# Expert products half in split fp32r parts, half in native fp32, with other buffers, one-hots and pacing

## The chip, the cores and the metric

The kernel runs on one core of a Trainium2 chip. It is judged by the device time of one execution in microseconds (us). A plain run gives one such time; a run with the hardware profiler gives one as well, and with it the span from the first to the last instruction and the trace that the rows below are taken from.

## The reference

One layer of a transformer for 256 tokens of width 2048, in fp32: two attention branches (a low-rank one and a differential one), gates, an output projection, and then an expert mixer. The change lies in the mixer alone. Its 16384 experts stand on a grid of 128 rows and 128 columns. Each token picks 16 experts in each of 8 heads, by two top-16 lists and a top-16 of their sums, and takes

```
h = rmsnorm(x, g_norm2)
...                                   # row, col, gates of 8 x 16 experts a token
experts = row * PEER_NKEYS + col
a = gelu(einsum('chkd,cd->chk', expert_u[experts], h))
w = gates * a
out = einsum('chk,chkd->cd', w, expert_v[experts])
```

`expert_u` and `expert_v` are 16384 x 2048 fp32, 134 MB each.

## The kernel before

**Stages.** Attention, gates and projections come first (0 to 810 us of the profile). Then the U stage (810 to 1520 us), then the V stage (1520 to 2147 us). For 192 of the 256 tokens (TD) the mixer is dense: every expert's product with every token is made, and a gate matrix that is zero where a token did not pick the expert is multiplied in. For the other 64 tokens (TG) the chosen rows are gathered from HBM: 128 gathers of 128 rows of 8 KB, 64 of U and 64 of V, spread over both stages.

**U stage.** A loop over 128 blocks of 128 experts. A block is one matrix of 2048 x 128 (1 MB), fetched in two tiles of 512 KB. `u_mm` multiplies it in 16 k tiles of 128 rows into one PSUM bank: the block's tile is the stationary operand, the normalized tokens `h2` (192 columns) the moving one. Both are plain fp32, which TensorE takes as it is ("native"). `u_evac` then applies Gelu on ScalarE from PSUM into `Blow` or `Bhigh`, which keep all 128 blocks. A one-element copy on VectorE, `pace`, marks that the block is done; gathers are tied behind it (`gather_to`).

**Work beside the blocks.** Three routing steps a block (top-16 lists, candidates, indices; VectorE) run from block 2 on. After half of them the gathers start. From block C0 = 32 on, 48 gate steps `g_step` are spread over the matmuls by GRATE: each multiplies, for 4 tokens, a one-hot matrix R of the rows (GpSimd) with a one-hot matrix C of the columns times the gates (VectorE), 4 matmuls of 128 columns, and VectorE multiplies the result into `Blow` and `Bhigh` or copies it there. GU = 80/128 of the gathers lie in the U stage. A gather's 128 rows are multiplied with `hrep` (U) or added to `gacc` (V) by one instruction on VectorE, and the buffer's next gather is issued on GpSimd behind it; there are two such buffers.

**Fetching and splitting.** Weights elsewhere, and all of V, are taken in two parts: `split` has ScalarE round a fetched tile `raw` to fp32r (`hi`), and VectorE subtract it (`lo`); fp32r matmuls of `hi` and `lo` follow. `fetch` gives such a tile one of three `raw` buffers, or for every fourth tile a fourth one. All fetches stand on one queue, SP's, in a fixed order; an issue that waits for a buffer holds up those behind it. In the U stage nothing is split, so `fetch_whole` uses the idle `hi` and `lo` buffers for fetches too: ten buffers of 512 KB, five blocks.

The order of instructions on an engine is set when the program is built; each engine, and SP's queue, works through its own list in order.

Of the kernel before, what the change touches and what calls it, by code (L numbers as in the profile page):

```python
# [7 lines left out]
F32 = mybir.dt.float32  # L8
F32R = mybir.dt.float32r
U32 = mybir.dt.uint32  # L10
AF = mybir.ActivationFunctionType
ALU = mybir.AluOpType
# [5 lines left out]
KD = D // 128  # L18
# [4 lines left out]
TD = 192  # L23
TG = T - TD
NLOW = 64
C0 = 32
NG4 = TD // 4
GRATE = NG4 / (88 * 16)
NEG = -1.0e30
NEGBIG = -3.0e38  # L30

# [1 line left out]
def hybrid_peer(tc, a, out):  # L33
    nc = tc.nc
    es = ExitStack()

    def pool(stack, name, bufs=1, side=None, space=None):
        kw = {} if space is None else dict(space=space)
        return stack.enter_context(
            tc.tile_pool(name=name, bufs=bufs, side=side, reuse_waits="tile", **kw))  # L40

    cst = pool(es, "cst")
    st = pool(es, "st")

    ident = cst.tile([128, 128], F32, name="ident")
    iota = cst.tile([128, 128], F32, name="iota")
    ones = cst.tile([128, 1], F32, name="ones")
    nhalf = cst.tile([128, 2], F32, name="nhalf")

    state = {"n": 0, "max": 3, "fill": 0, "b": 0, "g": 0, "c": 0, "f": 0, "s": 0, "w": 0}  # L50
    st2 = []


    def fetch(src):
        state["f"] += 1
        p, n = (st2[0], 1) if st2 and state["f"] % 4 == 3 else (st, 3)
        raw = p.tile([128, 1024], F32, tag="raw", name="raw", bufs=n)
        nc.sync.dma_start(raw, src)
        return raw

    def fetch_whole(src):

        i = state["w"] % (10 if st2 else 8)
        state["w"] += 1
        tag, n = (("raw", 3), ("hi", 3), ("lo", 2), ("raw", 3), ("hi", 3), ("raw", 3), ("hi", 3),
                  ("lo", 2), ("raw", 1), ("lo", 1))[i]
        p = st2[0] if i > 7 else st
        raw = p.tile([128, 1024], F32 if tag == "raw" else F32R, tag=tag, name="raw", bufs=n)
        raw = raw.bitcast(F32) if tag != "raw" else raw
        nc.sync.dma_start(raw, src)  # L70
        return raw

    def split(raw):

        hi = st.tile([128, 1024], F32R, tag="hi", name="hi", bufs=3)
        nc.scalar.activation(hi, raw, AF.Copy)  # L76
        state["s"] += 1
        p, n = (st2[0], 1) if st2 and state["s"] % 3 == 2 else (st, 2)
        lo = p.tile([128, 1024], F32R, tag="lo", name="lo", bufs=n)
        state["lo"] = nc.vector.tensor_sub(lo, raw, hi.bitcast(F32)).ins  # L80
        return hi, lo
# [36 lines left out]
    def tick(n=1):  # L118
        state["n"] += n
        if state["n"] >= TICK:  # L120
            state["n"] -= TICK
            advance()
# [48 lines left out]
    def ps_blk(n=3):  # L171
        state["b"] += 1
        return bank(f"b{state['b'] % n}")

    def ps_s():
        return pp.tile([128, 512], F32, tag="s", name="s", bufs=2)

    def ps_m():
        return pp.tile([128, 512], F32, tag="m", name="m", bufs=1)

    def w1(name, tag, bufs=2):
        return wk.tile([128, T], F32, tag=tag, name=name, bufs=bufs)
# [51 lines left out]
    g1, g2 = small[:, 0:16], small[:, 16:32]  # L234
# [157 lines left out]
    ps = ps_s()  # L392
# [23 lines left out]
    for h in range(NH):  # L416
        ps = ps_blk()
# [4 lines left out]
    for j in range(NH // 2):  # L422
        ps = ps_blk()
# [90 lines left out]
    for h in range(NH):  # L514
        ps = ps_blk()
# [55 lines left out]
    for b in range(32):  # L571
        ps = ps_blk()
# [15 lines left out]
    for j in range(KD):  # L588
        m = []
        for u, o, b in ((u_oa, oTa, j), (u_ob, oTb, 16 + j)):  # L590
            ps = ps_blk()
            block(u, o, NH, ps)
            mm = w1("mm", "rb", 3)
            nc.vector.scalar_tensor_tensor(mm, gt[:, b], 1.0, total(mm, ps),
                                           op0=ALU.add, op1=ALU.mult)
# [9 lines left out]
    gw = pool(gws, "gw", side="right")  # L605
    rowT = gw.tile([128, 2, 128], F32, name="rowT")
    colT = gw.tile([128, 2, 128], F32, name="colT")
    gateT = gw.tile([128, 2, 128], F32, name="gateT")

    hrep = gw.tile([128, D], F32, name="hrep")  # L610
    gidx = gw.tile([128, 64], U32, name="gidx")
# [5 lines left out]
    nc.gpsimd.tensor_add(sel[:, 64:128], ident[:, 0:64], ident[:, 64:128])  # L617
    h2s = ExitStack()
    h2p = pool(h2s, "h2p", side="right")
    h2 = h2p.tile([128, KD, TD], F32, name="h2")  # L620


    scs = ExitStack()
# [18 lines left out]
    def r2_job():  # L642
        yield
        v = nm.col()
        yield
        nc.scalar.activation(r2, nm.row(v), AF.Copy)
        yield
        for q in range(4):
            pt = ps_m()
            for i in range(4):  # L650
                k = 4 * q + i
                hn = w1("hn", "on", 3)
                nc.vector.tensor_mul(hn, xT[:, k], r2)
                nc.scalar.activation(h2[:, k], hn[:, 0:TD], AF.Copy, scale=g2[:, k:k + 1])
                hg = wk.tile([128, 2, TG], F32, tag="hg", name="hg", bufs=2)
                nc.gpsimd.tensor_scalar(hg, hn[:, TD:].unsqueeze(1).broadcast_to([128, 2, TG]),
                                        g2[:, k:k + 1], None, op0=ALU.mult)
                nc.tensor.transpose(pt[:, i * 128:(i + 1) * 128],
                                    hg.rearrange("p a t -> p (a t)"), ident)
                if i % 2:  # L660
                    yield
            nc.scalar.activation(hrep[:, q * 512:(q + 1) * 512], pt, AF.Copy)

    for j in range(KD):
        ps = ps_blk()
# [23 lines left out]
    for b in range(16):  # L689
        ps = ps_blk()  # L690
        block(u_wq, hu, KD, ps)
        job(score_job(b, ps))
    fill = []
    u_raw = []


    def u_mm(ps):
        for k in range(KD):
            if k % 8 == 0:
                u_raw.append(fetch_whole(a["eu"][len(u_raw)]))  # L700
            mm = nc.tensor.matmul(ps[:, 0:TD], lhsT=u_raw[-1][:, k % 8 * 128:(k % 8 + 1) * 128],  # L701
                                  rhs=h2[:, k], start=(k == 0), stop=(k == KD - 1),
                                  skip_group_check=True)
            state["u"] = mm.ins
            if active or queue:
                state["mm"] = mm.ins
                tick()
            state["fill"] += len(fill) > 0
            while fill and state["fill"] * GRATE >= NG4 + 1 - len(fill):
                fill.pop(0)()  # L710
# [14 lines left out]
    utp = pool(bs, "utp")  # L725
# [19 lines left out]
    for tb in (1, 0):  # L745
# [58 lines left out]
        def r_tr(env=env, tb=tb):  # L804
            pg = ps_g()
            for n, key in enumerate((0, 1, "g")):
                nc.tensor.transpose(pg[:, n, :], env[key].rearrange("p h k -> p (h k)"), ident)
            for n, dst in enumerate((rowT, colT, gateT)):
                nc.vector.tensor_copy(dst[:, tb, :], pg[:, n, :])

        steps.append(r_alloc)
        steps += [lambda b=b, f=r_list: f(b) for b in range(16)]
# [69 lines left out]
    def u_evac(c, ps):  # L882

        b = Bsl(c, c + 1)[:, 0]
        n = 4 * state["g"]
        if n < TD:
            nc.scalar.activation(b[:, n:], ps[:, n:TD], AF.Gelu_apprx_tanh)
        if n:
            t = utp.tile([128, TD], F32, tag="ut", name="ut", bufs=2)
            nc.scalar.activation(t[:, 0:n], ps[:, 0:n], AF.Gelu_apprx_tanh)  # L890
            nc.gpsimd.tensor_mul(b[:, 0:n], b[:, 0:n], t[:, 0:n])  # L891
        state["c"] = c + 1
        pace = utp.tile([128, 1], F32, tag="pace", name="pace", bufs=2)
        state["pace"] = nc.vector.tensor_copy(pace, b[:, TD - 1:TD] if n < TD else ps[:, 0:1]).ins  # L894

# [2 lines left out]
    def onehots(t4):  # L900
        rc = []
        for i in range(4):
            tb, tt = divmod(4 * t4 + i, 128)
            R = gp.tile([128, 128], F32, tag="R", name="R", bufs=12)
            C = gp.tile([128, 128], F32, tag="C", name="C", bufs=12)
            row, col, gate = [x[:, tb, tt:tt + 1] for x in (rowT, colT, gateT)]
            nc.gpsimd.tensor_scalar(R, iota, row, None, op0=ALU.is_equal)  # L907
            nc.vector.tensor_scalar(C, iota, col, gate, op0=ALU.is_equal, op1=ALU.mult)  # L908
            rc.append((R, C))
        RC[t4] = rc  # L910

# [17 lines left out]
                nc.vector.tensor_copy(bv, g)  # L929
        state["g"] += 1  # L930

    GU0, GU = 14, 80 / 128
    for c in range(C0):
        ps = ps_u() if c else ps0
        if c:
            u_mm(ps)
        u_evac(c, ps)
        for _ in range(3):
            if steps and c > 1:
                steps.pop(0)()  # L940
                if len(steps) == 34:
                    gather()
                    gather()
        gather_to(max(0, c - GU0) / (NB - GU0) * GU, state["pace"])
# [9 lines left out]
    fill += [lambda t4=t4: g_step(t4) for t4 in range(NG4)]  # L954
    for c in range(C0, NB):
        ps = ps_u()
# [84 lines left out]
    for half in range(2):  # L1041
# [17 lines left out]
        for c in range(NB):  # L1059
            raw = fetch(a["ev"][half, c])  # L1060
            hl = split(raw)
            parts = [[p[:, q * 512:(q + 1) * 512] for p in hl] for q in range(2)]
            w = weights(c)
# [143 lines left out]
```

## Time and profile before

| | |
|---|---|
| median of 3 runs | 2153.38 us (2150.89 to 2154.23) |
| profiled execution, its own time | 2148.66 us |
| its span | 2146.9 us |
[...]
| TensorE, VectorE, ScalarE, GpSimd busy | 98%, 67%, 37%, 27% of the span |

The page of the profile gives the busy time of each engine over the span, and again in 40 slices, in tenths. The chain of waits follows the work that ended last back to the start. Views of one line or one stretch give the durations of its instructions, what they waited for, and, for fetches, the time from issue to landing.

### The profile page before, as it was taken

What the parts mean: (1) busy time and instruction counts of PE and PEld (TensorE: products, weight loads), DVE (VectorE), ACT (ScalarE), POOL (GpSimd) and SP (SyncE); (2) the same over time, 40 slices, a digit from 0 to 9 for tenths busy, and PEclk for the clock granted to TensorE, in tenths of its full rate; (3) what the DMA queues carried; (4) which work ended last, traced back from release to release, by engine and by line L of the source; (5) the groups of instructions that cost most, each with busy time, mean ns of one, the idle gap of its engine ahead of it and who ended that gap; (6) DMA issues with size and microseconds to landing.
All of it is one profiled execution on the core that took longest, in us unless ns stands there. A gap on an engine that the chain in (4) does not pass through costs nothing.

```text
span 2146.9 us, 30521 instructions
## 1 busy us (share of the span) xinstructions
PE 2099.1 (98%) x11438; PEld 1864.9 (87%) x11438; DVE 1441.8 (67%) x2468; ACT 788.8 (37%) x1304; POOL 579.2 (27%) x525
## 2 busy tenths in 40 slices
PE   7989999999999999999999999999999999999998
PEld 6877778888888889999999999999888888788886
DVE  7666658666876798644555555554688878788874
ACT  3434437555554541100000000000355555555554
POOL 4121110000002302234666676663211111111100
PEclk9999999999999999999999999999999999999999
DMA  5453453455556557799888888888888888888874
GB/s 186 168 172 132 138 185 129 152 191 187 192 186 215 184 178 265 231 356 328 317 311 318 315 313 320 313 316 307 313 331 307 321 316 305 305 328 316 305 290 148
DMA packets 132708, 546.78 MB, mean 255 GB/s; under 512 B 15120, under 2 KB 15696, under 8 KB 116048
## 3 DMA queue, kind: packets, MB, share of 16 engines
q1 hardware_dynamic: 112032, 404.60, 53.0%
q0 software_dynamic: 18560, 134.29, 16.7%
q10 hardware_dynamic: 1968, 5.94, 0.9%
q8 instruction: 90, 1.47, 0.3%
q14 instruction: 58, 0.48, 0.1%
HBM read 537.89 MB, written 4.19 MB: 252 GB/s over the span
## 4 chain that ended last, share of the span: by engine, by line
PE 88%; DMA 2%; DVE 1%; issue 0%; ACT 0%; POOL 0%; ACTq 0%; DVEq 0%; POOLq 0%; SPq 0%
PE b L701 16%; PE b L137 15%; PE s L999 8%; PE b L139 8%; PE n L701 8%; PE m L701 8%; PE m L999 5%; PE n L999 5%; PE b L999 4%; PE t L999 4%; PE s L917 2%; DMA raw<-in_ev 1%; DVE lo L80 1%; PE b L156 1%; PE b L157 1%; PE b L155 1%
## 5 line engine op out<-in xcount | busy, mean ns | idle before, releaser
L80 DVE TENSOR_TENSOR lo<-raw,hi 128x1024 fp32r<-128x1024 f32 x502 | 635.0, 1270 | 269.7 <-ACT hi L76 129.7
L76 ACT ACTIVATE hi<-raw 128x1024 fp32r<-128x1024 f32 x502 | 531.9, 1061 | 537.1 <-PE n L999 139.2
L701 PE MATMUL b<-h,raw 128*128 128x192 f32 x2048 | 342.0, 326 | 0.0
L701 PEld LDWEIGHTS b<-h,raw 128*128 128x128 f32 x2048 | 333.1, 190 | 0.0
L137 PE MATMUL b<-xg,hi 128*128 128x512 f32 x912 | 328.0, 402 | 2.7 <-DVE xg L187 1.5
L139 PE MATMUL b<-xg,lo 128*128 128x256 f32 x912 | 259.2, 284 | 12.1 <-DVE lo L80 12.1
L137 PEld LDWEIGHTS b<-xg,hi 128*128 128x128 f32 x912 | 173.8, 191 | 46.6 <-issue 4.9
L999 PE MATMUL s<-hi,wt 128*128 128x512 f32 x512 | 203.1, 397 | 0.0
L139 PEld LDWEIGHTS b<-xg,lo 128*128 128x128 f32 x912 | 174.6, 191 | 14.0 <-DVE lo L80 13.8
L701 PE MATMUL n<-h,raw 128*128 128x192 f32 x1024 | 173.3, 326 | 0.0
L701 PE MATMUL m<-h,raw 128*128 128x192 f32 x1024 | 173.3, 326 | 0.0
L842 POOL DMA_INDIRECT rows<-in_evn,gidx x64 | 85.9, 1342 | 306.0 <-DVE gacc L860 276.2
L701 PEld LDWEIGHTS m<-h,raw 128*128 128x128 f32 x1024 | 166.9, 190 | 0.0
L701 PEld LDWEIGHTS n<-h,raw 128*128 128x128 f32 x1024 | 166.9, 190 | 0.0
L855 DVE SCALAR_TENSOR_TENSOR rows<-rows,hrep 128x2048 f32<-128x2048 f32 x64 | 148.7, 2324 | 14.3 <-DMA rows<-in_eun,gidx 14.3
L860 DVE SCALAR_TENSOR_TENSOR gacc<-rows,gwt,gacc 128x2048 f32<-128x2048 f32 x63 | 148.2, 2353 | 0.6 <-DVE pace L894 0.6
L907 POOL TENSOR_SCALAR R<-iota,rowT 128x128 f32<-128x128 f32 x192 | 136.0, 720 | 42.6 <-PE s L917 40.6
L842 POOL DMA_INDIRECT rows<-in_eun,gidx x64 | 75.8, 1184 | 255.6 <-DVE rows L855 196.3
L891 POOL TENSOR_TENSOR Bhigh<-Bhigh,ut 128x192 f32<-128x192 f32 (+28 forms) x64 | 97.9, 1529 | 88.6 <-ACT ut L890 81.2
L999 PEld LDWEIGHTS s<-hi,wt 128*128 128x128 f32 x512 | 96.3, 188 | 23.8 <-issue 0.5
L908 DVE TENSOR_SCALAR C<-iota,colT,gateT 128x128 f32<-128x128 f32 x192 | 62.9, 380 | 60.6 <-PE s L917 60.3
L999 PE MATMUL b<-hi,wt 128*128 128x512 f32 x256 | 102.1, 399 | 0.6 <-DVE wt L984 0.6
(316 smaller groups left out, 3502.9 us busy)
## 6 DMA issues: line engine op xcount, KB each, us to landing
raw<-in_eu SPq DMA_DIRECT2D x256, 512.0 KB, 5.4
raw<-in_ev SPq DMA_DIRECT2D x256, 512.0 KB, 4.6
raw<-in_w_in SPq DMA_DIRECT2D x133, 512.0 KB, 3.7
raw<-in_w_out SPq DMA_DIRECT2D x32, 512.0 KB, 4.3
raw<-in_w_q SPq DMA_DIRECT2D x32, 512.0 KB, 3.8
raw<-in_w_o_mla SPq DMA_DIRECT2D x16, 512.0 KB, 4.3
raw<-in_w_o_diff SPq DMA_DIRECT2D x16, 512.0 KB, 4.3
raw<-in_w_uq SPq DMA_DIRECT2D x9, 512.0 KB, 4.4
```

The costliest lines, as they stand in the source:

```text
L76: nc.scalar.activation(hi, raw, AF.Copy)
L80: state["lo"] = nc.vector.tensor_sub(lo, raw, hi.bitcast(F32)).ins
L137: nc.tensor.matmul(ps[0:m, 0:512], lhsT=hi, rhs=act[:, k, :], start=(k == 0), stop=False)
L139: state["mm"] = nc.tensor.matmul(ps[0:m, 0:256], lhsT=lo, rhs=act[:, k, 0:256], start=False, stop=(k == nk - 1)).ins
L701: mm = nc.tensor.matmul(ps[:, 0:TD], lhsT=u_raw[-1][:, k % 8 * 128:(k % 8 + 1) * 128], rhs=h2[:, k], start=(k == 0), stop=(k == KD - 1), s ...
L842: nc.gpsimd.indirect_dma_start(out=g, out_offset=None, in_=a["eun" if which == "u" else "evn"], in_offset=bass.IndirectOffsetOnAxis(ap=gid ...
L855: nc.vector.scalar_tensor_tensor(g, g, 1.0, hrep, op0=ALU.mult, op1=ALU.mult, accum_out=gdot[:, j:j + 1])
L860: nc.vector.scalar_tensor_tensor(gacc, g, gwt[:, j:j + 1], gacc, op0=ALU.mult, op1=ALU.add)
L891: nc.gpsimd.tensor_mul(b[:, 0:n], b[:, 0:n], t[:, 0:n])
L907: nc.gpsimd.tensor_scalar(R, iota, row, None, op0=ALU.is_equal)
L908: nc.vector.tensor_scalar(C, iota, col, gate, op0=ALU.is_equal, op1=ALU.mult)
L999: nc.tensor.matmul(o, lhsT=l, rhs=r, start=first and i == 0, stop=last and i == len(ops) - 1, skip_group_check=True)
```

## The change

- Of each block's 16 k tiles, the lower 8 (the first tile of 512 KB) are split by `split` and multiplied in two fp32r passes: `hi` with the high and low part of the tokens side by side (`h2hl`, 384 columns), `lo` with the high part (192 columns). The upper 8 stay native. PSUM then holds 384 columns a block.
- `u_evac` therefore copies the second 192 columns out on ScalarE (`us`), adds the first on VectorE, and takes Gelu from there. That add takes the place of `pace`.
- `fetch_whole` goes. U's fetches use `fetch`: the three `raw` buffers and the fourth.
- The token parts of k 0 to 7 are made by `split_scaled` (one more VectorE instruction each).
- C is made by two ScalarE instructions (an absolute difference, then a Relu with the gate as bias and the negated gate as scale) in place of one on VectorE.
- Two routing steps a block in place of three, gate steps from block 40 (C0) over 80 blocks, the start of gathers at block 20 in place of 14 (GU0), and 68/128 of them in the U stage (GU).

```diff
-C0 = 32
+C0 = 40
 NG4 = TD // 4
-GRATE = NG4 / (88 * 16)
+GRATE = NG4 / (80 * 16)
...
-    def fetch_whole(src):
-
-        i = state["w"] % (10 if st2 else 8)
-        state["w"] += 1
-        tag, n = (("raw", 3), ("hi", 3), ("lo", 2), ("raw", 3), ("hi", 3), ("raw", 3), ("hi", 3),
-                  ("lo", 2), ("raw", 1), ("lo", 1))[i]
...
-    h2 = h2p.tile([128, KD, TD], F32, name="h2")
+    h2hl = h2p.tile([128, KD // 2, 2 * TD], F32R, name="h2hl")
+    h2 = h2p.tile([128, KD // 2, TD], F32, name="h2")
...
-                nc.scalar.activation(h2[:, k], hn[:, 0:TD], AF.Copy, scale=g2[:, k:k + 1])
+                if k < KD // 2:
+                    split_scaled(h2hl[:, k], hn[:, 0:TD], g2[:, k:k + 1], TD)
+                else:
+                    nc.scalar.activation(h2[:, k - KD // 2], hn[:, 0:TD], AF.Copy,
+                                         scale=g2[:, k:k + 1])
...
     def u_mm(ps):
         for k in range(KD):
             if k % 8 == 0:
-                u_raw.append(fetch_whole(a["eu"][len(u_raw)]))
-            mm = nc.tensor.matmul(ps[:, 0:TD], lhsT=u_raw[-1][:, k % 8 * 128:(k % 8 + 1) * 128],
-                                  rhs=h2[:, k], start=(k == 0), stop=(k == KD - 1),
-                                  skip_group_check=True)
+                u_raw.append(fetch(a["eu"][len(u_raw)]))
+                hl = split(u_raw[-1]) if k == 0 else None
+            ks = slice(k % 8 * 128, (k % 8 + 1) * 128)
+            if hl:
+                nc.tensor.matmul(ps[:, 0:2 * TD], lhsT=hl[0][:, ks], rhs=h2hl[:, k],
+                                 start=(k == 0), stop=False, skip_group_check=True)
+                mm = nc.tensor.matmul(ps[:, 0:TD], lhsT=hl[1][:, ks], rhs=h2hl[:, k, 0:TD],
+                                      start=False, stop=False, skip_group_check=True)
+            else:
+                mm = nc.tensor.matmul(ps[:, 0:TD], lhsT=u_raw[-1][:, ks], rhs=h2[:, k - 8],
+                                      start=False, stop=(k == KD - 1), skip_group_check=True)
...
+        us = utp.tile([128, TD], F32, tag="us", name="us", bufs=2)
+        nc.scalar.activation(us, ps[:, TD:2 * TD], AF.Copy)
+        state["pace"] = nc.vector.tensor_add(us, us, ps[:, 0:TD]).ins
+        ps = us
...
-        pace = utp.tile([128, 1], F32, tag="pace", name="pace", bufs=2)
-        state["pace"] = nc.vector.tensor_copy(pace, b[:, TD - 1:TD] if n < TD else ps[:, 0:1]).ins
...
-            nc.vector.tensor_scalar(C, iota, col, gate, op0=ALU.is_equal, op1=ALU.mult)
+            nc.scalar.activation(C, iota, AF.Abs, bias=col, scale=-1.0)
+            nc.scalar.activation(C, C, AF.Relu, bias=gate, scale=ng)
...
-    GU0, GU = 14, 80 / 128
+    GU0, GU = 20, 68 / 128
...
-        for _ in range(3):
+        for _ in range(2):
```

SP's queue of fetches early in the U stage, before. `L70` is the issue in `fetch_whole`; what stands in brackets is the semaphore of the engine or queue whose work the issue waits for (DMAHW: an earlier fetch into the same buffer; PE: the matmuls that read it last).

```order
L70 DMA raw_7508<-in_eu 128x1024 [waits PE_49]
L70 DMA raw_7518<-in_eu 128x1024 [waits PE_49]
L70 DMA raw_7592<-in_eu 128x1024 [waits DMAHW2_49,PE_49]
L70 DMA raw_7602<-in_eu 128x1024 [waits DMAHW4_49,DMAHW3_49,PE_49]
L70 DMA raw_7634<-in_eu 128x1024 [waits DMAHW6_49,PE_49]
L70 DMA raw_7644<-in_eu 128x1024 [waits DMAHW5_49,PE_49]
L70 DMA raw_7676<-in_eu 128x1024 [waits DMAHW7_49,PE_49]
```

Every fetch waits for matmuls, those of the tile that lay in its buffer ten fetches earlier. The same place after the change (`L58` is the issue in `fetch`). In these rows raw_7551 and raw_7573 are the lower and upper tile of block 3, 7600 and 7622 of block 4, 7649 and 7671 of block 5, 7698 and 7720 of block 6, 7747 the lower tile of block 7, and 7796 that of block 8.

```order
L58 DMA raw_7600<-in_eu 128x1024 [waits DVE_49]
L58 DMA raw_7551<-in_eu 128x1024 [waits DMAHW2_49,PE_49]
L58 DMA raw_7573<-in_eu 128x1024 [waits DMAHW7_49,DVE_49]
L58 DMA raw_7622<-in_eu 128x1024 [waits DMAHW4_49,PE_49]
L58 DMA raw_7698<-in_eu 128x1024 [waits DMAHW6_49,DVE_49]
L58 DMA raw_7649<-in_eu 128x1024 [waits DMAHW5_49,PE_49]
L58 DMA raw_7671<-in_eu 128x1024 [waits DMAHW3_49,DVE_49]
L58 DMA raw_7720<-in_eu 128x1024 [waits DMAHW0_49,PE_49]
L58 DMA raw_7796<-in_eu 128x1024 [waits DMAHW2_49,DVE_49]
L58 DMA raw_7747<-in_eu 128x1024 [waits DMAHW1_49,PE_49]
```

The waits now alternate between matmuls and VectorE's `lo`. By the counts that they wait for: the lower tile of an odd block b waits for the last matmul of block b - 3; the upper tile of an odd block b waits for `lo` of the same block, since it is given the buffer of that block's lower tile; the upper tile of an even block b waits for the last matmul of block b - 3; the lower tile of an even block b waits for `lo` of block b - 2 (the fourth buffer serves these alone). This pattern repeats every two blocks through the stage, but for a few places where an upper tile of an odd block gets a buffer that matmuls free.

ScalarE in the U stage before, while no gate steps run, does one Gelu a block from the block's bank.

```order
L887 ACTIVATE Blow_7426<-m_7443 128x192 [waits PE_49]
L887 ACTIVATE Blow_7426<-n_7467 128x192 [waits PE_49]
L887 ACTIVATE Blow_7426<-b0_7507 128x192 [waits PE_49]
L887 ACTIVATE Blow_7426<-b1_7549 128x192 [waits PE_49]
L887 ACTIVATE Blow_7426<-m_7591 128x192 [waits PE_49]
```

After, the banks b0_7550, b1_7599 and m_7648 are blocks 3, 4 and 5.

```order
L64 ACTIVATE hi_7651<-raw_7649 128x1024 [waits DMAHW3_49]
L64 ACTIVATE hi_7700<-raw_7698 128x1024 [waits DMAHW2_49,PE_49,Activation_49]
L891 ACTIVATE us_7583<-b0_7550 128x192 [waits PE_49,Activation_49]
L895 ACTIVATE Blow_7448<-us_7583 128x192 [waits DVE_49]
L891 ACTIVATE us_7632<-b1_7599 128x192 [waits PE_49,Activation_49]
L895 ACTIVATE Blow_7448<-us_7632 128x192 [waits DVE_49]
L64 ACTIVATE hi_7749<-raw_7747 128x1024 [waits DMAHW7_49]
```

The splits of blocks 5 and 6 now stand as a pair ahead of the evacuation of block 3, and the next pair behind that of block 4. On VectorE the two `lo` of a pair stand together in the same way.

## Rows read from the trace of the kernel before

**Rows 1.** The page: busy time of engines, and the span in 40 slices.

```profile
PE 2099.1 (98%) x11438; PEld 1864.9 (87%) x11438; DVE 1441.8 (67%) x2468; ACT 788.8 (37%) x1304; POOL 579.2 (27%) x525
PE   7989999999999999999999999999999999999998
PEclk9999999999999999999999999999999999999999
```

**Rows 2.** Busy time by stretch: U without gathers, U with them, V.

```profile
core 0: us, PE busy (x) PEld busy (x) DVE busy (x) ACT busy (x) POOL busy (x), PEclk, DMA share, GB/s
...
815.00:845.00 30.00, 30.00 (x188) 30.00 (x187) 23.70 (x85) 6.53 (x11) 13.94 (x12) 1.00 0.63 210
850.00:1500.00 650.00, 650.00 (x4124) 649.96 (x4123) 341.07 (x743) 48.23 (x210) 358.80 (x368) 1.00 0.87 314
1550.00:2050.00 500.00, 498.05 (x2149) 400.84 (x2148) 407.26 (x486) 271.76 (x326) 71.74 (x44) 1.00 0.83 315
```

**Rows 3.** Chain of waits in the U stage, in order of time: start, length.

```profile
816.38 5.20 PE m L701 x32
821.58 5.20 PE n L701 x32
826.78 10.40 PE b L701 x64
```

**Rows 4.** U's matmuls, by the bank they write: first and last start.

```profile
L701 PE MATMUL b<-h,raw x2048: 326/326/328, 810.6 to 1520.0; 128*128 128x192 f32 x187
```

**Rows 5.** TensorE's timeline around one gate step.

```profile
987.83 1.05 PE L917 MATMUL s<-C,R 128*128 128x128 f32 x8
988.72 0.82 PE L701 MATMUL m<-h,raw 128*128 128x192 f32 x4
```

**Rows 6.** TensorE's timeline in a split stage: fp32r, 512 and 256 columns.

```profile
618.60 0.40 PE L137 MATMUL b<-mT,hi 128*128 128x512 f32 x1
618.84 0.28 PE L139 MATMUL b<-mT,lo 128*128 128x256 f32 x1
618.96 0.39 PE L137 MATMUL b<-mT,hi 128*128 128x512 f32 x1
```

**Rows 7.** U's fetches without gathers, 815 to 845 us: issues, and issue to landing.

```profile
L70 SPq DMA_DIRECT2D raw<-in_eu x11: 327/328/328, 816.0 to 842.4; - x11
...
DMA to landing us min/median/max: 4.3/4.4/4.7
```

**Rows 8.** Two fetches issued close together, 807 to 808.3 us.

```profile
L70 SPq DMA_DIRECT2D raw<-in_eu x2: 328/378/427, 807.5 to 807.9; - x2
...
DMA to landing us min/median/max: 4.8/5.2/5.7
```

**Rows 9.** U's fetches among gathers, 900 to 1500 us.

```profile
L70 SPq DMA_DIRECT2D raw<-in_eu x213: 327/328/328, 899.9 to 1494.3; - x107
...
DMA to landing us min/median/max: 3.5/5.8/10.0
```

**Rows 10.** The page: DMA queues. q0 carries the 128 gathers, q1 SP's fetches.

```profile
q1 hardware_dynamic: 112032, 404.60, 53.0%
q0 software_dynamic: 18560, 134.29, 16.7%
```

**Rows 11.** Chain of waits at the start of V: one fetch behind a split.

```profile
1524.86 1.04 ACT hi L76
1525.90 0.02 issue
1525.92 1.24 DVE lo L80
1527.16 0.02 issue
1527.18 7.13 DMA raw<-in_ev
```

**Rows 12.** SP's queue: whom U's issues waited for, 820 to 1500 us.

```profile
SPq L70 <- PE b L701: 272.1, 114, 3.1
```

**Rows 13.** Instructions by line, duration min/median/max: `lo` beside GpSimd's rope, then R.

```profile
L80 DVE TENSOR_TENSOR lo<-raw,hi x53: 1217/1226/3396, 103.2 to 298.7; 128x1024 fp32r<-128x1024 f32 x53
L907 POOL TENSOR_SCALAR R<-iota,rowT x192: 591/602/2729, 947.6 to 1449.9; 128x128 f32<-128x128 f32 x192
```

**Rows 14.** Groups of instructions by line and shape: busy time, mean of one.

```profile
L860 DVE SCALAR_TENSOR_TENSOR gacc<-rows,gwt,gacc 128x2048 f32<-128x2048 f32 x63 | 148.2, 2353 | 0.6 <-DVE pace L894 0.6
L908 DVE TENSOR_SCALAR C<-iota,colT,gateT 128x128 f32<-128x128 f32 x192 | 62.9, 380 | 60.6 <-PE s L917 60.3
L464 ACT ACTIVATE sc<-sc,mx 128x128 f32<-128x128 f32 x24 | 9.6, 399 | 22.7 <-DVE mx L463 22.6
L145 DVE TENSOR_TENSOR mm<-mm,b 128x256 f32<-128x256 f32 x32 | 13.3, 417 | 4.1 <-ACT mm L144 3.9
L144 ACT ACTIVATE mm<-b 128x256 f32<-128x256 f32 x32 | 11.7, 367 | 0.0
```

More of the change, by code (lines that the diff above doesn't have):

```diff
@@ L48, in hybrid_peer @@
     nhalf = cst.tile([128, 2], F32, name="nhalf")
-    state = {"n": 0, "max": 3, "fill": 0, "b": 0, "g": 0, "c": 0, "f": 0, "s": 0, "w": 0}
+    state = {"n": 0, "max": 3, "fill": 0, "b": 0, "g": 0, "c": 0, "f": 0, "s": 0}
     st2 = []
@@ L57, in fetch @@
         raw = p.tile([128, 1024], F32, tag="raw", name="raw", bufs=n)
-        nc.sync.dma_start(raw, src)
-        return raw
-    def fetch_whole(src):
-        i = state["w"] % (10 if st2 else 8)
-        state["w"] += 1
-        tag, n = (("raw", 3), ("hi", 3), ("lo", 2), ("raw", 3), ("hi", 3), ("raw", 3), ("hi", 3),
-                  ("lo", 2), ("raw", 1), ("lo", 1))[i]
-        p = st2[0] if i > 7 else st
-        raw = p.tile([128, 1024], F32 if tag == "raw" else F32R, tag=tag, name="raw", bufs=n)
-        raw = raw.bitcast(F32) if tag != "raw" else raw
         nc.sync.dma_start(raw, src)
@@ L608, in hybrid_peer @@
     gateT = gw.tile([128, 2, 128], F32, name="gateT")
+    ngateT = gw.tile([128, 2, 128], F32, name="ngateT")
     hrep = gw.tile([128, D], F32, name="hrep")
@@ L809, in r_tr @@
                 nc.vector.tensor_copy(dst[:, tb, :], pg[:, n, :])
+            nc.scalar.activation(ngateT[:, tb, :], pg[:, 2, :], AF.Copy, scale=-1.0)
         steps.append(r_alloc)
@@ L905, in onehots @@
             C = gp.tile([128, 128], F32, tag="C", name="C", bufs=12)
-            row, col, gate = [x[:, tb, tt:tt + 1] for x in (rowT, colT, gateT)]
+            row, col, gate, ng = [x[:, tb, tt:tt + 1] for x in (rowT, colT, gateT, ngateT)]
             nc.gpsimd.tensor_scalar(R, iota, row, None, op0=ALU.is_equal)
-            nc.vector.tensor_scalar(C, iota, col, gate, op0=ALU.is_equal, op1=ALU.mult)
+            nc.scalar.activation(C, iota, AF.Abs, bias=col, scale=-1.0)
+            nc.scalar.activation(C, C, AF.Relu, bias=gate, scale=ng)
             rc.append((R, C))
```

## The prediction

> **What bounds the kernel now.** I read the page first, then the stretches, the chain, and last the queues. TensorE is busy all the way at full clock [rows 1], and the stretches say so stage by stage: in the U stage it works 650 of 650 us, in V 498 of 500 [rows 2]. In the U stage VectorE has 341 of 650 us and ScalarE 48 of 650, so both have room; DMA is at 0.87 there, at 314 GB/s. The chain runs through U on TensorE alone, one block after the other, 5.20 us each [rows 3]: 16 k tiles, so 0.325 us a native product of 192 columns. A gate step takes 988.72 - 987.83 = 0.89 us more [rows 5]. Sum for U: 128 x 5.20 + 48 x 0.89 = 708.3 us; the trace has 810.6 to 1520.0, and the last instruction [rows 4]. No fetch is late: SP's queue waits for matmuls to free a buffer [rows 12], up to 3.1 us at a time, never the other way round.
>
> So U is bound by TensorE, and V too. All that follows is about U's 708 us and what could take TensorE's place.
>
> **What the change saves on TensorE.** Fp32r products of 512 and 256 columns follow each other after 0.24 and 0.12 us [rows 6]. For 384 columns I take what lies between, 0.18. For 192 columns fp32r no row exists: from below 0.09 (in proportion to 256), from above 0.325 (the native price of the same 192 columns). I take 0.12, the nearest row. A pair is then 0.30 against 0.325, and a block 8 x 0.30 + 2.60 = 5.0 us; with 0.09 it is 4.76. I go on with 4.9: on TensorE alone 128 x 0.30 = 38 us less.
>
> **What it adds beside TensorE.** A block gets a `hi` (1.04) and a `lo` (1.24) [rows 11], a copy of 192 columns on ScalarE and an add on VectorE (below 0.37 and 0.42, the 256-column rows [rows 14]). C moves: 192 x 0.38 us leave VectorE, 384 instructions of at most 0.40 come to ScalarE [rows 14]. VectorE's share goes from 0.52 to about 0.65, ScalarE's from 0.07 to about 0.5. As sums these are hidden behind TensorE. The dropped `pace` copies and the later gate steps cost or save nothing there, since the 48 gate steps stay.
>
> Where they stand is the point. ScalarE has the split of block b behind the evacuation of block b - 3, and VectorE the same; both only sit waiting for the tile to land, with nothing of TensorE's behind them but evacuations, for which there are four banks. That wait is free as long as the tile comes in time.
>
> **What it does to the fetches.** Here the margin goes. Before, ten buffers held five blocks; now four hold two, and the upper tile of an odd block is issued only when `lo` of its own lower tile is done (the SP rows of the change). Let x be the end of `lo` of odd block b. At x SP issues, in order: upper b; upper b + 1 right behind it (its buffer was free, but its place in the queue is behind); lower b + 3 after the pair's second `lo`, at x + 1.24; lower b + 2, when block b - 1 is through. The upper tile of b lands 4.4 us after x without gathers [rows 7], and TensorE needs it for the second half of b, so block b - 1 ended at the latest 4.4 - 2.3 = 2.1 us after x: all four are issued within some 2 us. Transfers of one queue pass one after another: issues at 807.5 and 807.9 landed 4.8 and 5.7 us later, so at 812.3 and 813.6, 1.3 us apart [rows 8]. Lower b + 2, the last, lands at x + 4.4 + 3 x 1.3 = x + 8.3. Then `hi`, `lo` and 0.1 for hand-overs (the V rows show exactly this sequence, 0.02 between its members [rows 11]): x' = x + 8.3 + 1.04 + 1.24 + 0.1 = x + 10.7.
>
> A loop of 10.7 us for two blocks, which nothing in TensorE shortens. TensorE needs 2 x 4.9 = 9.8 without gate steps, 10.6 with them (108 blocks hold 48, so 0.79 for two blocks). Before, two blocks took 10.4, and with gate steps, over the same 108 blocks, (108 x 5.20 + 42.7) / 54 = 11.2.
>
> **Gathers in the loop.** From block 20 on, 68 gathers in 108 blocks make 1.26 in two blocks. Each moves 134.29 / 128 = 1.05 MB [rows 10], two tiles' worth, 2.6 us of the DMA engines. What of it falls between x and the landing of lower b + 2 lengthens the loop; the rest fills the 2.4 us of the split and the latency ahead of the next burst. Bounds: 0, and all of it, 1.26 x 2.6 = 3.3 us. The nearest row is what gathers did to U's fetches before: median landing 5.8 against 4.4 us, 1.4 us more [rows 7, 9]. I take 1.4: a loop of 12.1 us, 6.05 us a block.
>
> **A lock that I leave out of the sum.** `lo` is steady at 1.23 us but took up to 3.40 where GpSimd's rope ran, and GpSimd's R is 0.60 but took up to 2.73, about one gather instruction of VectorE (2.35) plus itself [rows 13, 14]. So the two engines sometimes wait for each other's whole instruction. A `lo` that waits for half an R (0.3 us) in each loop costs 54 x 0.3 = 16 us. [...] I keep the 16 us for the range, since the median `lo` beside GpSimd was not longer.
>
> **The sum**, against the profiled execution's own 2148.66 us: blocks 0 to 19, 10.7 / 2 = 5.35 against 5.20, +3 us; 108 blocks at 6.05, 653 against 604, +49; 12 more gathers in V, 12 x 2.35 = 28 us of VectorE, which has 407 of 500 us there and stays below TensorE, so 2 of them for late splits; the eight extra VectorE instructions before U, below 0.42 each, nothing. Together +54: 2203 us for that execution. It lies 4.7 under the median of the runs, so against the median 2207 us.
>
> **The rivals.**
> 1. The loop stays hidden and TensorE sets the pace, so it becomes faster. It decides at the gathers' share: with the 5 us lost elsewhere the loop must stay 0.1 us under the 11.2 of before, so gathers may add at most 0.4 of their 3.3 us. For it: a gather is issued when VectorE is done with a row buffer, and VectorE does that behind the `lo` pair, so its data may come just in the gap of the burst. Against it: landings spread from 3.5 to 10.0 us among gathers before [rows 9]. With no gather in the burst the loop is 10.7: 54 x (11.2 - 10.7) = 27 less, 3 and 2 back, 2131 by the median; the whole 38 would give 2117. Chance 0.2.
> 2. Fp32r of 192 columns costs what native costs. Then a pair is 0.18 + 0.325 = 0.505, a block 6.64, two with gate steps 14.1, longer than the loop; 128 x 1.44 = 184 more, 2339. For it: no fp32r product under 256 columns stands in the trace. Against it: from 512 to 256 columns the price just halves [rows 6]. Chance 0.1.
> 3. It comes out even: gathers add 0.3 to 0.5. Within 0.2% (4.3 us, about what a measurement of this kernel can tell) of 2153.4. Chance 0.1.
> 4. My forecast, the loop with gathers in it: 0.6. Its own range is 2160 to 2300; all gathers in the burst make it 14.0 us a loop, 54 x 2.8 + 5 = 156 more, 2310.
>
> **How the numbers follow.** Slower by over 0.2%: 0.6 + 0.1 = 0.7; same 0.1; faster 0.2. The range runs from 2125, which holds most of rival 1, to 2300, which holds the loop with nearly all gathers and leaves out rival 2: some 0.2 left out.
>
> **What the profile after would show.** Right: TensorE idle in U, 0.5 to 1 us a block, released by a fetch or by `lo` and `hi`; the chain going through raw<-in_eu, `hi` and `lo` in turns; SP's queue waiting for `lo`; the blocks' starts about 12 us apart by twos, and about 10.7 before the first gather; a pair of products at 0.27 to 0.30. Wrong: TensorE without gaps in U, at 4.9 us a block (rival 1), or without gaps at 6.6 (rival 2). The forecast fails if the four transfers of a burst don't queue, if gathers fall into its gap, or if another wait of U (the gate steps' one-hots on ScalarE, the evacuations behind the `lo` pair) ends later than the fetch.

## The result, and the profile after

The changed kernel took 2211.2 us (median of 6 runs, 2202.8 to 2217.7) against 2153.3 us for the kernel before beside it: 1.0267 times as long, interval 1.0239 to 1.0294. The profiled execution took 2204.57 us, with a span of 2202.8. The page of the kernel after, busy time and 40 slices, against [rows 1]:

```profile
PE 2080.1 (94%) x11438; PEld 1844.8 (84%) x11438; DVE 1558.1 (71%) x2412; ACT 1080.8 (49%) x1938; POOL 572.3 (26%) x517
PE   7989999999999997889999999999899999999998
...
DVE  7666658556876668955566666666678888788885
```

TensorE is busy 19 us less than before in a span that is 56 us longer: it now stands still, above all in slices 16 to 18 (826 to 991 us), U's first blocks. VectorE is at 8 and 9 in the first two of them. The same by windows (columns as in [rows 2]):

```profile
815.00:845.00 30.00, 23.58 (x153) 22.81 (x152) 30.00 (x157) 8.11 (x15) 0.00 (x0) 1.00 0.39 136
820.00:880.00 60.00, 44.16 (x254) 42.20 (x254) 54.44 (x206) 16.38 (x28) 13.02 (x10) 0.91 0.35 128
...
850.00:1500.00 650.00, 597.27 (x3843) 587.55 (x3842) 416.90 (x727) 314.61 (x791) 316.84 (x343) 0.97 0.76 273
1600.00:2100.00 500.00, 491.77 (x2167) 404.76 (x2166) 426.13 (x502) 269.89 (x325) 90.23 (x55) 0.99 0.87 336
```

Before, the first 30 us of this were TensorE 30.00 and VectorE 23.70 [rows 2]. Now VectorE is busy 30.00 of 30 and TensorE 23.58: the two have changed places. Whom TensorE waited for, blocks 0 to 39 (811 to 1071 us), then blocks 40 to 127 (to 1574):

```profile
PE b L705 <- DMA raw<-in_eu: 12.2, 8, 2.3
PE b L702 <- DVE lo L68: 11.6, 4, 4.6
PE m L705 <- DMA raw<-in_eu: 10.2, 9, 2.4
PE m L702 <- DVE lo L68: 8.1, 3, 3.1
PE b L700 <- ACT hi L64: 1.8, 2, 1.4
...
PE m L705 <- DMA raw<-in_eu: 11.7, 8, 3.1
PE b L705 <- DMA raw<-in_eu: 8.4, 8, 3.0
PE b L702 <- DVE lo L68: 0.6, 1, 0.6
```

43.9 us in the first 40 blocks, 20.7 in the other 88. Behind some waits the granted clock was lower: TensorE stood 2.78 us for `lo` before 855.76 us, and from 857 to 867 us it was granted 0.50:

```profile
855.76 0.36 PE L702 MATMUL b<-h2hl,lo 128*128 128x192 f32 x1 [2.78 <-DVE lo L68]
857.00:867.00 10.00, 8.04 (x27) 7.69 (x27) 8.50 (x23) 3.46 (x5) 5.41 (x5) 0.50 0.55 206
```

There are five such stretches before block 40, some 34 us together; U of before had none. A wait of 3.08 us before 841.3 us was followed by none (1.00 from 840 to 856).

From the times at which blocks begin I made this table for all kernels (us; the first two blocks are left out; "after U" is from U's last matmul to the end of the span):

| kernel | blocks 2-9 | 10-19 | 20-29 | 30-39 | 40-127 | U in all | after U |
|---|---|---|---|---|---|---|---|
| before | 41.6 | 52.3 | 52.3 | 55.6 | 497.1 | 709.8 | 626.6 |
| **after** | 60.7 | 67.8 | 63.1 | 59.0 | 502.9 | 763.7 | 628.4 |
| e1 routing paced | 39.5 | 61.8 | 54.7 | 75.3 | 507.5 | 749.0 | 626.4 |
| e2 rest alone | 41.6 | 52.2 | 52.2 | 52.3 | 500.6 | 709.8 | 641.6 |
| e3 five buffers | 63.0 | 72.0 | 59.3 | 53.6 | 484.9 | 743.0 | 618.4 |
| e5 gathers still | 61.4 | 67.0 | 60.6 | 52.9 | 481.1 | 733.2 | 614.4 |
| e6 both | 39.1 | 57.5 | 58.0 | 72.9 | 490.4 | 728.2 | 618.3 |
| e7 late transposes | 39.1 | 55.3 | 60.2 | 66.9 | 488.3 | 720.0 | 616.6 |
| e9 ScalarE's queue | 39.1 | 48.9 | 62.8 | 59.7 | 486.1 | 706.8 | 622.1 |
| e10 gathers later | 39.1 | 49.2 | 55.2 | 50.2 | 490.4 | 694.4 | 622.3 |
| e12 weights +192 B | 41.6 | 52.3 | 52.3 | 55.6 | 497.1 | 709.8 | 615.7 |
| e13 after, weights +64 B | 60.8 | 67.3 | 64.2 | 61.1 | 506.8 | 770.5 | 644.9 |

U lost 54 us where 52 were forecast, but 48 of them before block 40. What stands there on VectorE shows in its timeline (start, length, engine, line):

```profile
834.73 0.41 DVE L765 TENSOR_TENSOR cand<-v 128x256 f32<-128x256 f32 x1
835.06 0.28 DVE L743 MAX8 v<-scr 128x8 f32<-128x128 f32 x1
835.27 0.40 DVE L740 MAX8 cs<-cand 128x8 f32<-128x256 f32 x1
835.59 0.33 DVE L892 TENSOR_TENSOR us<-us,n 128x192 f32<-128x192 f32 x1
...
839.73 0.41 DVE L740 MAX8 cs<-cand 128x8 f32<-128x256 f32 x1
840.06 2.34 DVE L68 TENSOR_TENSOR lo<-raw,hi 128x1024 fp32r<-128x1024 f32 x2
```

and ScalarE's behind it:

```profile
835.96 0.36 ACT L895 ACTIVATE Blow<-us 128x192 f32<-128x192 f32 x1 [7.35 <-DVE us L892]
836.22 1.99 ACT L64 ACTIVATE hi<-raw 128x1024 fp32r<-128x1024 f32 x2
```

The add of a block's sum (L892) stands in VectorE's list behind routing instructions (MAX8, `cand`, ...). ScalarE waits 7.35 us for it with its Gelu, behind which stand the two `hi`; when these end at 838.2, VectorE is at the next routing steps until 840.06, and only then comes to `lo`, without which TensorE can't go on. The source asks for two steps a block, four for a pair of `lo`; VectorE's list has 9, 5, 7, 10 and 9 between the six pairs from 824 to 905 us. That ScalarE kept to the order of its list shows here: the DMA engines moved nothing from 834 to 842 us (share 0.00), so the tiles of the two `hi` were there by 834, and the first of them, which waits for its fetch alone (`hi_7651`), still began only at 836.22, behind the Gelu.

### The profile page after: what moved, and what is told of

It is laid out like the page before. It is cut to its first block, busy times and chain, and to the rows that moved or that the text cites. A ratio compares the mean times of both kernels' runs of the same rounds, so it can differ in the third digit from the quotient of the medians.

```text
span 2202.8 us, 31317 instructions
## 1 busy us (share of the span) xinstructions
PE 2080.1 (94%) x11438; PEld 1844.8 (84%) x11438; DVE 1558.1 (71%) x2412; ACT 1080.8 (49%) x1938; POOL 572.3 (26%) x517
## 4 chain that ended last, share of the span: by engine, by line
PE 65%; DMA 14%; DVE 7%; issue 3%; ACT 2%; POOL 1%; SPq 0%; ACTq 0%; DVEq 0%; POOLq 0%
PE b L125 15%; DMA raw<-in_eu 11%; PE b L127 8%; PE s L1006 7%; PE m L1006 5%; PE n L1006 5%; PE b L1006 4%; PE b L705 4%; PE t L1006 4%; DVE lo L68 3%; PE b L700 2%; PE m L705 2%; ACT hi L64 2%; PE n L705 2%; DMA raw<-in_ev 2%
## 5 line engine op out<-in xcount | busy, mean ns | idle before, releaser
L68 DVE TENSOR_TENSOR lo<-raw,hi 128x1024 fp32r<-128x1024 f32 x630 | 789.7, 1263 | 482.8 <-ACT hi L64 314.1
L64 ACT ACTIVATE hi<-raw 128x1024 fp32r<-128x1024 f32 x630 | 660.0, 1059 | 728.7 <-PE n L1006 200.2
L705 PE MATMUL b<-h,raw 128*128 128x192 f32 x1024 | 188.6, 338 | 20.6 <-DMA raw<-in_eu 20.6
L705 PEld LDWEIGHTS b<-h,raw 128*128 128x128 f32 x1024 | 171.7, 197 | 25.0 <-DMA raw<-in_eu 24.9
L700 PE MATMUL b<-h2hl,hi 128*128 128x384 f32 x512 | 164.6, 383 | 1.8 <-ACT hi L64 1.8
L913 POOL TENSOR_SCALAR R<-iota,rowT 128x128 f32<-128x128 f32 x192 | 145.0, 768 | 10.6 <-PE s L924 4.8
L702 PE MATMUL b<-h2hl,lo 128*128 128x192 f32 x512 | 131.6, 257 | 12.2 <-DVE lo L68 12.1
L705 PE MATMUL m<-h,raw 128*128 128x192 f32 x512 | 95.0, 339 | 21.9 <-DMA raw<-in_eu 21.9
L702 PEld LDWEIGHTS b<-h2hl,lo 128*128 128x128 f32 x512 | 100.8, 197 | 13.9 <-DVE lo L68 13.9
L705 PEld LDWEIGHTS m<-h,raw 128*128 128x128 f32 x512 | 86.1, 197 | 26.0 <-DMA raw<-in_eu 26.0
L899 POOL TENSOR_TENSOR Bhigh<-Bhigh,ut 128x192 f32<-128x192 f32 (+28 forms) x64 | 71.4, 1118 | 122.0 <-ACT ut L898 121.3
```

What stands on the lines that cost most here:

```text
L700: nc.tensor.matmul(ps[:, 0:2 * TD], lhsT=hl[0][:, ks], rhs=h2hl[:, k], start=(k == 0), stop=False, skip_group_check=True)
L702: mm = nc.tensor.matmul(ps[:, 0:TD], lhsT=hl[1][:, ks], rhs=h2hl[:, k, 0:TD], start=False, stop=False, skip_group_check=True)
L705: mm = nc.tensor.matmul(ps[:, 0:TD], lhsT=u_raw[-1][:, ks], rhs=h2[:, k - 8], start=False, stop=(k == KD - 1), skip_group_check=True)
```

## The experiments

Theory A: the loss is VectorE's list. Theory B: the prediction's fetch loop with gathers in it.

**e1: the routing steps tied to the block that names them.**

```diff
             if steps and c > 1:
-                steps.pop(0)()
+                with tc.issue_after(state["pace"]):
+                    steps.pop(0)()
```

> The changed kernel with one edit: on VectorE each routing step of blocks 2 to 39 is tied behind the add of the block after which the source names it, so that the program can no longer place ten steps between two pairs of `lo`. Theory A (VectorE's list: the routing instructions stand ahead of the block's add and of `lo` in blocks 0 to 40, which took 260.8 us for 40 blocks against 212.7 before): those blocks come back to 5.0 to 5.4 us each, 40 to 55 us less, about 2165 us. Theory B (the prediction's fetch loop with gathers in it, in blocks 20 to 127): the loop stays as it is, at most 10 us less, 2201 to 2211 us.

2189.8 us, 1.0157 of before [1.0119, 1.0196]. Blocks 2 to 9 fell from 60.7 to 39.5 us, 4.94 each, TensorE's own pace (window 820 to 862):

```profile
820.00:862.00 42.00, 41.84 (x274) 41.61 (x273) 27.78 (x120) 13.02 (x24) 0.00 (x0) 1.00 0.53 198
```

So theory A holds for these blocks. But blocks 0 to 39 got back 19.3 us only: now the loop shows behind block 10, and the steps end so late that the transposes on TensorE wait for them:

```profile
PE s L810 <- DVE res L805: 11.1, 2, 7.0
```

The loop can be read here undisturbed, from SP's issues of U's tiles (count, length, first and last start):

```profile
L58 SPq DMA_DIRECT2D raw<-in_eu x4: 327/328/383, 823.3 to 826.9; - x4
L58 SPq DMA_DIRECT2D raw<-in_eu x4: 327/328/383, 833.9 to 836.7; - x4
L58 SPq DMA_DIRECT2D raw<-in_eu x4: 328/328/384, 844.0 to 846.5; - x4
L58 SPq DMA_DIRECT2D raw<-in_eu x4: 328/356/385, 855.1 to 856.6; - x4
```

Four fetches at a time, (855.1 - 823.3) / 3 = 10.6 us apart. The forecast said 10.7. Two blocks of TensorE take 9.88 us in this stretch, so it draws on tiles fetched earlier; behind block 10 the fetches are late (in blocks 0 to 39 TensorE waits 11.4 us for them).

**e2: everything but the split, with native U and its ten buffers.**

```diff
-C0 = 32
+C0 = 40
-    GU0, GU = 14, 80 / 128
+    GU0, GU = 20, 68 / 128
...
+            nc.scalar.activation(C, iota, AF.Abs, bias=col, scale=-1.0)
+            nc.scalar.activation(C, C, AF.Relu, bias=gate, scale=ng)
```

> The kernel before with everything of the change but the split of U's lower tiles: gates from block 40, two routing steps a block, fewer gathers in U, C made on ScalarE; U native, with its ten buffers. Both theories put the loss on the split, so they expect 2148 to 2160 us. A third theory (the later gates and the 12 gathers moved into V cost the time by themselves) expects 2170 us or more.

2164.8 us, 1.0055 [1.004, 1.0071], between the two expectations. U is the same to the tenth, 709.8: later gates and one-hots on ScalarE cost U nothing. After U 15.0 us are lost; 10.0 of them are waits of TensorE (13.5 against 3.5 before), above all for splits of V:

```profile
PE b L1002 <- DVE lo L80: 7.6, 7, 1.9
PE s L1002 <- ACT hi L76: 4.2, 1, 4.2
```

That the 12 gathers moved there are the reason is likely, but no run moved them alone.

**e3: five buffers for U's tiles, the upper ones in two of their own.**

```diff
+    def fetch_upper(src):
+        raw = st2[0].tile([128, 1024], F32, tag="rawu", name="raw", bufs=2)
...
-            R = gp.tile([128, 128], F32, tag="R", name="R", bufs=12)
+            R = gp.tile([128, 128], F32, tag="R", name="R", bufs=8)
```

> The changed kernel with U's lower tiles in three buffers and the upper ones in two of their own (one buffer more than now; room for it from R and C in 8 buffers each instead of 12 and one scratch tile for Gelu instead of two). No upper tile waits for `lo` of its own block any more. Theory B: the loop is gone, blocks 40 to 127 go from 5.72 to 5.3 us (what TensorE needs with gate steps), 35 us less, and blocks 0 to 40 gain as well: 2150 to 2175 us. Theory A: blocks 0 to 20 stay where VectorE is (54 of 60 us busy), at most 20 us less, 2190 us or more.

2174.6 us, 1.0099 [1.0064, 1.0135]. Each theory was right in its own place: blocks 40 to 127 fell by 18.0 us to 484.9 (B, half of the 35 expected), blocks 2 to 19 did not gain (A; 135.0 us against 128.5). The total falls by more than U does: the edit gives V a fifth buffer too, and after U this run takes 10.0 us less.

**e5: no gathered data after the first two** (e4, the same without its factor 0, gave no time).

```diff
+            if got["issued"] < 2:
+                g = gap.tile([128, D], F32, tag="rows", name="rows", bufs=2)
...
+            g = kept[got["issued"] % 2]
```

> The changed kernel with only the first two gathers' data moved: all later uses read the two row buffers again (with a factor 0 where they multiply in place), so VectorE's work for the gathered tokens stays and 126 gathers of 1.05 MB each are left out. (The output of the 64 gathered tokens is then not the reference's.) Theory B, by which gathers lengthen the fetch loop: blocks 40 to 127 go from 5.72 us to 5.3 to 5.4, what TensorE needs with gate steps, 30 us less. If instead the loop's length is its own (the split and four transfers behind one another), they stay above 5.6 us. By theory A blocks 2 to 20 keep their 128 us in either case.

2161.3 us, 1.0046 [1.0029, 1.0062]; its profile from 1080 to 1500 us:

```profile
1080.00:1500.00 420.00, 419.50 (x2839) 418.80 (x2839) 282.11 (x362) 252.35 (x672) 219.02 (x255) 1.00 0.56 193
```

TensorE is busy 419.5 of 420, 5.47 us a block, with the same four buffers and the same list on VectorE. So gathers do lengthen the loop: 502.9 - 481.1 = 21.8 us over 44 loops, at least 0.50 a loop, since in e5 TensorE and not the loop sets the pace. Blocks 2 to 19 keep 128.4 of their 128.5 us.

**e6 and e7: e1 and e3 together; then the transposes later too.**

```diff
+            late = r_tr
+        else:
+            steps.insert(-14, late)
+            steps += [lambda: None] * 4 + [r_tr]
```

> The two edits that each took one part of the loss away, together: routing steps tied behind the pace, and five buffers for U's tiles with the upper ones apart. If the two causes are separate, blocks 0 to 40 take 215 to 241 us (the paced run's 241.5, less what its late fetches cost) and blocks 40 to 128 about 485 us (the five-buffer run's); with U from 812 us on and 620 us for V that is 2135 to 2160 us. If they are one cause, it is no better than the better of the two, 2175 us.

> The same, with the transposes of the routing results (on TensorE, for which it waited 4.2 and 7.0 us in the paced run) taken nine blocks later for the first half of the tokens and two blocks later for the second. If those waits are real losses and no others stand behind them: 8 to 11 us less than the run with both edits. If the wait for VectorE's routing only moves, within 4 us of it.

2158.4 us, 1.0024 [1.0008, 1.004], and 2155.7, 1.0012 [0.9996, 1.0029]. The causes are two. The transposes' wait mostly moved on: e7 is 2.7 us better, within the two intervals, and TensorE waits 21.3 us for fetches in blocks 0 to 39 of e7. On SP's queue an upper tile stands behind a lower one that waits for a `lo`, and that `lo` stands behind paced routing steps.

**e9 and e10: the upper tiles issued from ScalarE's queue; then the gathers after the routing.**

```diff
-        nc.sync.dma_start(raw, src)
+        nc.scalar.dma_start(raw, src)
...
-    GU0, GU = 20, 68 / 128
+    GU0, GU = 39, 68 / 128
```

> The run with both edits and late transposes, with one more: the upper tiles are issued by ScalarE's queue instead of SP's, where each stands right behind the copy of a block's sum and waits for the same matmul. In the run without this edit TensorE still waited 31.7 us for fetches, most of it in blocks 10 to 40: on SP's queue the upper tile of block b stands behind the lower one of block b + 4, which waits for a `lo` behind routing steps. If that order is the cause, blocks 10 to 40 come from 182 to 155 to 165 us and the whole to 2125 to 2140 us. If VectorE itself is the limit there (188 us busy in the 221 us of blocks 2 to 40), the wait moves to `lo` and `hi` and it stays above 2148 us.

> The same as the run before this one with the 68 gathers of the U stage spread over blocks 39 to 127 instead of 20 to 127, so that VectorE has no gathered rows to work on (2.35 us each, 12 or 13 of them) beside the routing steps. If VectorE is what is left to limit blocks 20 to 40, these lose 15 to 30 us, and the blocks behind gain less than 5 back: 2105 to 2125 us. If not, it is within 5 us of the run before this one.

2135.4 us, 0.9922 [0.99, 0.9945], and 2120.0, 0.9858 [0.984, 0.9876]: faster than both kernels. But all runs made from the changed kernel, e13 apart, have V's weights at a place that saves 16 us in V (below). The kernel before with its weights moved alone (e12) is at 0.9922 as well, so against it e9 gains nothing and e10 0.6%. Windows of e9, then of e10, in the routing blocks:

```profile
866.00:1029.00 163.00, 147.30 (x912) 144.92 (x910) 146.90 (x400) 47.01 (x86) 44.52 (x33) 0.96 0.69 250
```

```profile
820.00:1013.00 193.00, 188.74 (x1218) 187.52 (x1218) 156.45 (x534) 67.33 (x119) 27.45 (x22) 0.99 0.61 212
```

In e9 blocks 10 to 19 run at TensorE's pace (48.9); from 866 us on VectorE is busy 0.90 of the time and TensorE still waits 15.6 us for fetches. Blocks 10 to 39 gained 11 us of the 17 to 27 expected. With the gathers moved behind the routing (e10) blocks 20 to 39 fell from 122.5 to 105.4, and TensorE works 188.7 of 193 us. That takes away both the gathers' rows from VectorE and their transfers (13 in blocks 20 to 39 of e9, 2 in e10); no run parts the two.

**e8, e11, e12, e13: where V's weights lie.** After U, changed kernel and before took nearly the same (628.4 and 626.6), though TensorE waits longer there after the change. Its products are closer: 227 ns from one to the next by the median, against 231 and 236 in turns, the same instructions. The tile of the weights (`wt`, the stationary operand) had moved by 1472 bytes, since `us` and `pace` differ in size.

```diff
             wp = pool(bs, "wp")
+            wp.tile([128, 16], F32, tag="pad", name="pad", bufs=1)
```

(16 floats for 64 bytes, 368 and 48 for 1472 and 192, in the kernel before; 16 in the changed one.)

> The kernel before with 64 bytes left free ahead of V's weights, nothing else. In V, TensorE's products of 512 columns stand 231 and 236 ns apart in turns in the kernel before and in the run of the rest alone, but 226 to 227 ns apart in the changed kernel and in both runs made from it; V's weights lie at a multiple of 128 bytes in the first two and at 64 bytes past one in the others. If that is the cause, V's products come 6.7 ns closer here, some 2400 of them, 16 us: 2137 us. If not, 2153 us.

> The kernel before with 1472 bytes left free ahead of V's weights, which puts them at the very address that they have in the changed kernel; the 64 bytes of the run before did not bring V's products closer. If the address itself sets their distance, they stand 226 to 227 ns apart here, 16 us less in V. If they stay at 231 and 236 ns in turns, the weights' place has nothing to do with it, and what makes V's products closer in the changed kernel stays open.

> The kernel before with 192 bytes left free ahead of V's weights. Counted from the last multiple of 256 bytes the weights then lie at 192, as they do in the changed kernel, in the five-buffer runs and in the run with 1472 bytes, all with V's products 227 ns apart; at 0 (before, the rest alone) and at 64 (64 bytes on) they were 233. If the place within 256 bytes decides: 227 ns and 2135 to 2139 us. If it is something else of the address: 233 ns and 2149 to 2157 us.

> The changed kernel with 64 bytes left free ahead of V's weights, which puts them at a multiple of 256 bytes, as in the kernel before. If the place within 256 bytes decides, V's products go from 227 to 233 ns and the time from 2211 to about 2227 us: then the change's own cost is some 74 us, of which the weights' new place gave 16 back by accident. If not, 2211 us.

64 bytes: 2151.2 us, 0.9993 [0.9979, 1.0007], nothing. 1472 bytes: 2136.5 (one run). 192 bytes: 2138.5, 0.9922 [0.9904, 0.9941]. The changed kernel with 64 more: 2224.8, 1.032 [1.0285, 1.0356]; its interval just touches that of the changed kernel, but after U it takes 16.5 us more and the products are back at 233 ns in the mean. Windows of e8, then e12, in V:

```profile
1550.00:2050.00 500.00, 498.01 (x2151) 400.49 (x2150) 404.95 (x483) 271.11 (x326) 69.19 (x43) 1.00 0.84 315
```

```profile
1550.00:2050.00 500.00, 495.06 (x2185) 407.87 (x2184) 412.67 (x494) 276.21 (x332) 70.61 (x44) 1.00 0.85 321
```

And e13, 492.40 / 2109 = 0.2335:

```profile
1620.00:2120.00 500.00, 492.40 (x2109) 394.94 (x2108) 419.73 (x496) 266.56 (x321) 89.55 (x55) 0.99 0.87 331
```

498.01 / 2151 = 0.2315 us a product against 495.06 / 2185 = 0.2266 ([rows 2] for before: 498.05 for 2149). My first guess, 64 bytes past a multiple of 128, failed (e8); the second, the place within 256 bytes, foretold e12 and e13.

## Why the prediction was right, and where it was not

The time was 2211 where I said 2207, with a loss in U of 54 us where I said 52. But the sum came out by errors that cancel. By stretches, against what the forecast gives: blocks 0 to 19, forecast 107.0, measured 138.7, 32 more; blocks 20 to 39, 121.0 and 122.1; blocks 40 to 127, 88 x 6.05 = 532 and 502.9, 29 less. That 20 to 39 agree is partly chance too: of TensorE's 17.5 us of waits there, 6.0 are for `lo` and `hi`. The signs that the forecast named fit in part only: two of the blocks 2 to 9 take 15.2 us where it said 10.7, and TensorE stands 0.24 us a block in blocks 40 to 127 (20.7 / 88) where it said 0.5 to 1.

**TensorE's saving: right.** The pair was taken as 0.30 us (0.18 and 0.12), and a block as 4.9. After:

```profile
816.33 0.36 PE L700 MATMUL m<-h2hl,hi 128*128 128x384 f32 x1
816.53 0.25 PE L702 MATMUL m<-h2hl,lo 128*128 128x192 f32 x1
816.62 0.36 PE L700 MATMUL m<-h2hl,hi 128*128 128x384 f32 x1
...
818.05 0.36 PE L700 MATMUL m<-h2hl,hi 128*128 128x384 f32 x1
```

Six pairs in 1.72 us: 0.287 each, 0.20 for 384 columns and 0.09 for 192. Undisturbed blocks (e6) take 39.1 / 8 = 4.89 us. Rival 2 (192 columns at native price) is false.

**The burst and the loop: right.** Four issues together, within 1.5 to 3.6 us in e1, after `lo` of an odd block; 10.6 us against 10.7. In the changed kernel:

```profile
L58 SPq DMA_DIRECT2D raw<-in_eu x4: 328/355/383, 825.6 to 827.2; - x4
L58 SPq DMA_DIRECT2D raw<-in_eu x4: 328/355/383, 841.3 to 842.8; - x4
```

Here, in blocks 2 to 9, it is 15.7 us long, since `lo` is late. SP's queue in U waits for it, as the forecast asked for, 77 times, and longer still for earlier fetches into the same buffers, which stand ahead of the `lo` in the same loop:

```profile
SPq L58 <- DMA raw<-in_eu: 369.5, 68, 8.7
SPq L58 <- DVE lo L68: 195.0, 77, 9.9
```

**Gathers in the loop: mechanism right, size wrong.** I took 1.4 us a loop, from the later landings among gathers [rows 7, 9], with a bound of 0 below. Blocks 40 to 127 run at 11.43 us for two instead of 12.1, and at 10.93 without the gathers' data (e5). There TensorE sets the pace, so 0.50 is the least that the gathers add; against the loop of 10.6 in e1 it is 0.8. The nearest row, a shift in a single fetch's landing, was two to three times too large for a chain of four.

**Hidden as sums: the step that failed.** "Both only sit waiting for the tile to land" is false in blocks 2 to 39. I divided VectorE's work over all of U (0.65), and did not read that part of its list, where routing stands ahead of the adds and of `lo`; before, nothing of TensorE's waited for it. e1 showed the cost: 21 us in blocks 2 to 9 alone. With the steps spaced as the source names them VectorE was busy 27.78 of 42 us there and TensorE 41.84, so in these blocks the order costs the time and not the amount. From block 10 on the amount is high even when spaced (146.90 of 163 us in e9).

Part of this amount came into U with the change. The section on the kernel before says that the routing steps run from block 2 on; that is where the source names them, but in the trace of before, as in e2, 21 of the 48 top-16 lists were begun before U, beside the projections, where TensorE sets the pace. After the change all 48 stand in U. VectorE from 700 to 811 us, before and after:

```profile
700.00:811.00 111.00, 108.50 (x644) 96.22 (x643) 93.18 (x263) 53.87 (x89) 20.02 (x20) 0.98 0.55 190
700.00:811.00 111.00, 109.40 (x659) 97.17 (x658) 67.55 (x100) 57.16 (x93) 24.93 (x20) 1.00 0.55 181
```

That is 25.6 us of VectorE's work that the forecast has nowhere. Why the list places it later once the lower tiles are split, and what blocks 10 to 39 would take without it, no run shows.

Rival 1, a faster kernel, fails on the order alone. With order, buffers, queue and gathers repaired (e10) U takes 694.4 us: of the 38 us forecast as TensorE's saving, 15 come through.

**V: the number right, its parts wrong.** I said 2 us for late splits; the profile has 1.8. It is 15.0 for what the rest of the change does there (e2), 18.3 with the weights at a multiple of 256 bytes as before (e13, 644.9 - 626.6), less 16.5 for the weights' place.

**The lock: rightly left out.** `lo` beside GpSimd's R, blocks 40 to 127:

```profile
L68 DVE TENSOR_TENSOR lo<-raw,hi x89: 1210/1224/1539, 1073.3 to 1573.1; 128x1024 fp32r<-128x1024 f32 x89
```

At most 0.3 us in one of them. R still reached 2.71: of the 16 R over 2.3 us, six lie beside a pair of `lo` and ten beside a gather's instruction on VectorE. If that is a lock, GpSimd pays it here; no wait of TensorE for R is in the trace.

## What to carry to other kernels

Before work is called hidden, divide it by the stage in which it stands, not by the loop that contains it, and read the list of the engine that gets it, before and after: a list set at build time can put work for later ahead of what TensorE needs next (21 us in blocks 2 to 9, e1), and a change can move work from one stage into another (25.6 us of VectorE's here). Where tiles passed through a split, a shared queue and shared buffers tied fetches to VectorE's list (195.0 us of waits of SP's queue for `lo`); give those that wait for TensorE a queue of their own (from 1.0012 to 0.9922 of before, e7 to e9). A forecast that hits the total is no proof of its terms; compare stage by stage.

## What the runs showed of the hardware

- The place of the weights in SBUF sets how close TensorE's fp32r products of 512 columns follow: 227 ns with V's weights at 192 bytes past a multiple of 256 (after, e11, e12), 233 in the mean at 0 and 64 (before, e8, e13). Over V this is 16 us, 0.8% of the kernel, for 192 bytes left empty. The place within 256 is only what these addresses have in common (the five-buffer runs lie at 192 too); why, and what other places give, stays open.
- A wait of 2.78 us on TensorE was followed by 10 us at a granted clock of 0.50 (window 857 to 867, with a second wait of 1.96 us inside). There 16 native products took 5.49 us (from 861.09), against 2.79 at 1.00 (from 850.02). Whether the wait brought the lower clock (after one of 3.08 us it stayed at 1.00), and how much of the time lost in U is due to it, no run shows.
